# A weight split issued behind a later copy, DMA weight sums moved five products up, and branch A's block sums moved into the convolution stage

## The chip, the cores and the metric

The kernel runs on one core of one Trainium2 chip. The metric is device microseconds of one execution. The profile is of one execution, taken by the hardware profiler; its engines are PE (matmul), PEld (weight load), DVE, ACT, POOL and SP. SP and POOL only issue DMAs here, apart from two multiplies at the end on POOL.

## The reference, cut to what matters

One layer of a bidirectional encoder over 1024 tokens of width 1024, in float32:

```python
x = x + 0.5 * swiglu(rmsnorm(x, ffn1_norm), ffn1_w_in, ffn1_w_out)      # width 2816
h = rmsnorm(x, mix_norm)
z = h @ w_in                               # columns u, v | gate_b, gate_c, xb | g_a, g_b
u, v = gelu(u), gelu(v)
y_a = (u * (W_s rmsnorm(v) + b)) @ w_proj_a          # branch A
y_b = (gate_b * conv3(gate_c * xb)) @ w_proj_b       # branch B
x = x + (sigmoid(g_a) * y_a + sigmoid(g_b) * y_b) @ w_out
x = x + 0.5 * swiglu(rmsnorm(x, ffn2_norm), ffn2_w_in, ffn2_w_out)
return rmsnorm(x, final_norm)
```

## The kernel before, in words

Every large product is computed on feature-major activations (128 features x 512 tokens a tile, two token halves). A float32 factor is cut into a rounded part and a remainder (`parts`, line 85: an ACT copy makes `hi`, a DVE subtraction makes `lo`), and three matmuls of 128 x 512 replace one: hi*hi, hi*lo, lo*hi.

Products of a 2 x 2 block of weights with a 2 x 2 block of activations are taken by a Strassen-like scheme with seven products instead of eight. A **group** (`group`, line 352) is one such block: it runs its products in the order 1, 7, 6, 2, 5, 3, 4 (`ORDER`; `SHORT`, line 32, puts 4 ahead of 3 for blocks of fewer than four tiles), each of n*3 matmuls, n being 4, 3 or 2. Product 2 is cut in two halves around product 5 where n is 4. Three PSUM banks serve a group: `ba` takes product 1, then 6, 5 and 3 are added onto it one after the other, and after each an ACT copy takes the running sum out: `t1` after product 1, `u2` after product 6, `u5` after product 5. PE cannot add product 6 onto `ba` until the `t1` copy has read it, nor product 5 until the `u2` copy has, nor product 3 until the `u5` copy has.

**Weights.** `plan` lists all weight blocks ("S" entries; "F" entries are computed without the scheme, "R" are the last ones). An S entry loads raw tiles of 128 x 2 x 512 through SP (`fetch_until`): `x_`, `y_` and, unless its flag `dve` is set, `z_`. Five such buffers exist (tag "wr"). The seven weight factors are sums of blocks. For entries without the flag three accumulating DMAs on POOL's queue make them (`add_to`, line 94: y0 += x0, z0 += y0, z1 += y1); for entries with it (the second matrix of each feed-forward part, and the three projections) DVE makes two of the three. A fourth sum, x1 += z0, is always an accumulating DMA, issued once `pair(x_, 1, 2)` has read x_. Then `parts` splits each pair into `wh`/`wl` buffers (three of each), and the fourth sum alone into `wh4`/`wl4` (one of each), for product 3.

`make_ready` walks over all products of all entries (`units`) in the order in which they are used, `AHEAD` = 5 products ahead of the one that is taken, so the fourth sum's split, which belongs to product 3, stands in program order where product 1 of the same group is taken (in `ORDER`), and the three DMA sums of the next entry where product 6 of this group is taken. Program order is not queue order: a planner lays all instructions out by priority (program position, moved up by `high_priority`) over a simulated run, and an instruction that is ready there can come to stand in its engine's queue ahead of earlier ones that are not. Each engine's queue then runs in order.

**Stages.** In order: feed-forward 1 in (`gu`), out (`o`), then the mixer: `v`, `u`, eight `cx` and four `gb` groups (the convolution, lines 994 to 1040: `cx`, `cx`, `gb` for each d), eight `gg` groups (sigmoid gates, from line 1043), `ya`, `yb`, `o`, then feed-forward 2. Activations that a later stage needs in scheme form are put into DRAM tiles (`Shelf`). Branch A's shelf `ad` gets only its blocks when the gated heads are made (`gate_heads`, line 964); its sums are made later by `Shelf.sums` (line 684), a generator that loads four tiles, makes four differences on DVE and stores them, in five steps for each of four tiles k. Before the change its steps run in the first four `gg` groups, one after each product (lines 1050 and 1054). `Shelved` (line 703) loads the finished sums for the `ya` stage during `gg`. `unhurried` (line 312) issues gain and square work behind the `t1` copy.

Of the kernel before, what the change touches and what calls it, by code (L numbers as in the profile page):

```python
# [14 lines left out]
P = 128  # L15
# [20 lines left out]
def kernel(ctx, tc, x, ffn1_norm, ffn1_w_in, ffn1_w_out, mix_norm, w_in,  # L36
# [128 lines left out]
    AHEAD_OF = 300  # L165
    AHEAD = 5
    at = [0, 0, 0]
    raws, ready = {}, {}
    kept, closing = [], []

    def raw_tile():
# [2 lines left out]
    def fetch_until(e):  # L174
        while at[2] < min(e, len(plan)):
# [17 lines left out]
                nc.sync.dma_start(raw.rearrange("p h c -> p (h c)"), s[1][s[2] * P:(s[2] + 1) * P, :])  # L193
            at[2] += 1

    def make_ready(n):
        while at[1] < min(n, len(units)):
            e, i = units[at[1]]
            if i == 0 and not closing:
                return  # L200
            fetch_until(e + 1)
            s, q = plan[e], raws[e]
            if i == 0:
                f = s[2] - LAST
                if f % 2 == 0:
                    kept.append((big("wah", F32R), big("wal", F32R)))
                hi, lo = (t[:, (f % 2) * 2:(f % 2) * 2 + 2, :] for t in kept[-1])
                parts(hi, lo, q)
                ready[at[1]] = hi, lo
            elif s[0] == "F":  # L210
                c = i == "Y"
                if e == 1:
                    hi, lo = (t[:, 2 * c:2 * c + 2, :] for t in places(6))
                else:
                    hi = wp.tile([P, 2, HT], F32R, tag="wh", name=nm("wh"))
                    lo = wp.tile([P, 2, HT], F32R, tag="wl", name=nm("wl"))
                parts(hi, lo, q[c])
                ready[at[1]] = hi, lo
            else:
                if i == 1 and s[7]:  # L220
                    q.append(raw_tile())
                x_, y_, z_ = q
                sz = s[4] * P

                def pair(src, first, second):
                    hi = wp.tile([P, 2, HT], F32R, tag="wh", name=nm("wh"))
                    lo = wp.tile([P, 2, HT], F32R, tag="wl", name=nm("wl"))
                    with tc.high_priority(offset=AHEAD_OF // 2):
                        parts(hi[:, :, :sz], lo[:, :, :sz], src[:, :, :sz])
                    for h, name in enumerate((first, second)):  # L230
                        ready[e, name] = hi[:, h, :], lo[:, h, :]

                if i == 1:
                    if s[7]:
                        nc.vector.tensor_tensor(z_[:, 1, :sz], y_[:, 0, :sz], y_[:, 1, :sz], ALU.add)
                        nc.vector.tensor_tensor(z_[:, 0, :sz], z_[:, 1, :sz], x_[:, 0, :sz], ALU.add)
                        add_to(y_[:, 0, :sz], x_[:, 0, :sz])
                    else:
                        add_to(y_[:, 0, :sz], x_[:, 0, :sz])
                        add_to(z_[:, 0, :sz], y_[:, 0, :sz])  # L240
                        add_to(z_[:, 1, :sz], y_[:, 1, :sz])
                    pair(x_, 1, 2)
                    add_to(x_[:, 1, :sz], z_[:, 0, :sz])
                elif i == 6:
                    pair(z_, 6, 5)
                elif i == 7:
                    pair(y_, 7, 4)
                elif i == 3:
                    hi = wp.tile([P, HT], F32R, tag="wh4", name=nm("wh4"), bufs=1)
                    lo = wp.tile([P, HT], F32R, tag="wl4", name=nm("wl4"), bufs=1)  # L250
                    parts(hi[:, :sz], lo[:, :sz], x_[:, 1, :sz])
                    ready[e, 3] = hi, lo
                ready[at[1]] = ready.pop((e, i))
            if i in (0, 1, "X"):
                fetch_until(e + 2 + (i == 0))
            at[1] += 1

    def take(n, ahead=AHEAD):

# [92 lines left out]
    def group(name, blk, use, after=None):  # L352

        n = blk.n
        e, i = units[at[0]]
        assert i == 1 and plan[e][4] == n
        if after is None:
            after = lambda i: None
        asked = use

        def use(*args):
            with tc.high_priority(offset=AHEAD_OF):
                asked(*args)

        def tt(*args):
            with tc.high_priority(offset=AHEAD_OF):
                nc.vector.tensor_tensor(*args)

        def copy(*args):
            with tc.high_priority(offset=2 * AHEAD_OF):  # L370
                return nc.scalar.copy(*args)  # L371

        t1, u2, u5 = act("t1"), act("u2"), act("u5")

        def product(i, ps, first=True):
            w, = take(1)
            term(ps, w, blk, i, range(n), first)

        split = n // 2 if n == KH else n
        ba, bb_, bc = bank(name), bank(name), bank(name)  # L380
        product(1, ba)
        unhurried(copy(t1, ba))
        after(1)
        product(7, bb_)
        after(7)
        product(6, ba, False)
        copy(u2, ba)
        after(6)
        w2, = take(1)
        term(bc, w2, blk, 2, range(split))  # L390
        if split == n:
            u3 = act("u3")
            tt(u3, bb_, u2, ALU.add)
            use(0, 0, bc, t1)
            after(2)
        product(5, ba, False)
        copy(u5, ba)
        use(1, 1, bb_, u5)
        after(5)
        if split < n:  # L400
            term(bc, w2, blk, 2, range(split, n))
            use(0, 0, bc, t1)
            after(2)
        else:
            bd = bank(name)
            product(4, bd)
            use(1, 0, bd, u3)
            after(4)
        product(3, ba, False)
        use(0, 1, ba, None)  # L410
        after(3)
        if split < n:
            product(4, bb_, False)
            use(1, 0, bb_, u2)
            after(4)
# [578 lines left out]
    def conv_tile(d, cv):  # L994

        cx = big("cx")
        seen = set()

        def use(i, b, ps, add):
            s = cx[:, 2 * i + b, :]  # L1000
            if i == 0:
                scaled(s, i, ps, add, rb2[b])
            else:
                total(s, i, ps, add)
            seen.add((i, b))
            if (1 - i, b) in seen:
                nc.vector.tensor_tensor(cx[:, b, :], cx[:, b, :], cx[:, 2 + b, :], ALU.mult)

        group("cx", blk, use, after=lambda i: gate_heads() if i == 6 else None)
        ts = [cx[:, b, :] for b in range(NB)]  # L1010
        for b in range(NB):
            y = cv[:, 2 * (d // KH) + b, :]
            nc.vector.tensor_scalar(y, ts[b], gain(5, d), None, ALU.mult)
            for g, o, i in ((4, 1, 0), (6, 0, 1)):
                nc.vector.scalar_tensor_tensor(y[:, o:o + HT - 1], ts[b][:, i:i + HT - 1], gain(g, d),
                                               y[:, o:o + HT - 1], ALU.mult, ALU.add)
            if b > 0:
                nc.vector.scalar_tensor_tensor(y[:, 0:1], ts[b - 1][:, HT - 1:HT], gain(4, d), y[:, 0:1],
                                               ALU.mult, ALU.add)
            if b < NB - 1:  # L1020
                nc.vector.scalar_tensor_tensor(y[:, HT - 1:HT], ts[b + 1][:, 0:1], gain(6, d), y[:, HT - 1:HT],
                                               ALU.mult, ALU.add)
            nc.vector.tensor_tensor(y, y, rb[b], ALU.mult)

    for d in range(KH):
        cv = big("cv")
        conv_tile(d, cv)
        conv_tile(d + KH, cv)

        def use(i, b, ps, add):  # L1030
            y = cv[:, 2 * i + b, :]
            if add is None:
                nc.vector.tensor_tensor(y, ps, y, ALU.mult)
            else:
                s = act("gb")
                total(s, i, ps, add)
                nc.vector.tensor_tensor(y, s, y, ALU.mult)
            bd.put(i, b, d, y)

        group("gb", blk, use)  # L1040


    for d in range(ND):
        def use(i, b, ps, add):
            s = act("sig")
            scaled(s, i, ps, add, rb[b])
            nc.scalar.activation(s, s, AF.Sigmoid)
            nc.sync.dma_start((sad, sbd)[i][d][b], s)

        steps = ad.sums(d) if d < KH else iter(())  # L1050
        if d == ND - 3:
            nxt = Shelved(ad, "a")
        if d < ND - 1:
            group("gg", blk, use, after=lambda i: next(steps, None))
        else:
            last_group("gg", blk, use, nxt)
    blk = nxt
# [198 lines left out]
```

## Time and profile before

| | us |
|---|---|
| three runs | 2195.01, 2195.36, 2199.61 (median 2195.36) |
| the profiled execution | 2196.39 |
| its span, first to last instruction | 2194.6 |
| PE busy in it | 2121.6 (97%) |
| DVE, ACT busy | 1368.7 (62%), 921.1 (42%) |
| TensorE's mean granted clock | 0.987 |

PE is the engine that bounds the kernel; the others matter where PE waits for them. "DMA" in a windows table is the mean busy share of the 16 DMA engines; it can come out a little above 1. The name of a group of instructions is output<-inputs: `wh<-wr` is the cast of a raw weight tile, with 128x1024 for a pair and 128x512, 128x384 or 128x256 for the fourth sum of a block of four, three or two tiles; `wr<-wr` on POOL is a DMA weight sum; `L371 COPY t` is the `t1` copy, `L371 COPY u` that of `u2` or `u5`.

### The profile page before, as it was taken

What the parts mean: (1) busy time and instruction counts of PE and PEld (TensorE: products, weight loads), DVE (VectorE), ACT (ScalarE), POOL (GpSimd) and SP (SyncE); (2) the same over time, 40 slices, a digit from 0 to 9 for tenths busy, and PEclk for the clock granted to TensorE, in tenths of its full rate; (3) what the DMA queues carried; (4) which work ended last, traced back from release to release, by engine and by line L of the source; (5) the groups of instructions that cost most, each with busy time, mean ns of one, the idle gap of its engine ahead of it and who ended that gap; (6) DMA issues with size and microseconds to landing.
All of it is one profiled execution on the core that took longest, in us unless ns stands there. A gap on an engine that the chain in (4) does not pass through costs nothing. (4 is left out here: it accounts for less than half of the span.)

```text
span 2194.6 us, 27089 instructions
## 1 busy us (share of the span) xinstructions
PE 2121.6 (97%) x9374; PEld 1741.7 (79%) x9374; DVE 1368.7 (62%) x1930; ACT 921.1 (42%) x1350; POOL 418.0 (19%) x486
## 2 busy tenths in 40 slices
PE   7999999999999989999998999999999999999987
PEld 6788888878877878888886878877788888888876
DVE  5855656576476455766663568586765555576566
ACT  5533333355356553222233445355433333354444
POOL 2111111112222111111111101212111111112313
PEclk9999999999999999999999999999999999999999
DMA  9577777989898556677799799868577677997962
GB/s 273 125 202 182 184 187 179 257 257 246 180 234 202 126 120 169 149 167 164 172 339 240 200 292 297 204 182 201 128 197 197 172 199 175 261 238 176 205 188 77
DMA packets 451247, 435.98 MB, mean 199 GB/s; under 512 B 26860, under 2 KB 313636, under 8 KB 451108
## 3 DMA queue, kind: packets, MB, share of 16 engines
q1 hardware_dynamic: 385604, 315.20, 44.8%
q0 software_dynamic: 65504, 119.04, 32.2%
q8 instruction: 73, 1.20, 0.2%
q14 instruction: 66, 0.54, 0.1%
HBM read 235.43 MB, written 100.66 MB: 153 GB/s over the span
## 5 line engine op out<-in xcount | busy, mean ns | idle before, releaser
L87 DVE TENSOR_TENSOR wl<-wr,wh 128x1024 fp32r<-128x1024 f32 (+3 forms) x420 | 441.8, 1055 | 616.8 <-ACT wh L87 601.6
L87 ACT CAST wh<-wr 128x1024 fp32r<-128x1024 f32 (+3 forms) x420 | 383.4, 919 | 599.8 <-DMA wr<-wr 318.1
L95 POOL DMA_DIRECT2D wr<-wr x342 | 296.2, 906 | 1519.3 <-DVE wl L87 557.0
L371 ACT COPY u<-gu 128x512 f32<-128x512 f32 x82 | 47.8, 583 | 188.5 <-PE gu L83 188.5
L580 DVE TENSOR_TENSOR gu<-gu,rb 128x512 f32<-128x512 f32 x120 | 78.9, 685 | 0.0
L95 POOL DMA_DIRECT2D xd<-o x64 | 56.6, 954 | 103.7 <-DVE o L99 33.6
L99 DVE SCALAR_TENSOR_TENSOR gu<-gu,u 128x512 f32<-128x512 f32 x82 | 56.3, 687 | 12.7 <-PE gu L83 7.9
L371 ACT COPY u<-o 128x512 f32<-128x512 f32 x54 | 31.4, 582 | 74.2 <-PE o L83 70.8
L83 PE MATMUL gu<-t1h,wh 128*128 128x512 f32 x180 | 50.5, 393 | 8.8 <-ACT t1h L87 8.8
L739 ACT ACTIVATE gu<-gu 128x512 f32<-128x512 f32 x88 | 54.6, 627 | 7.3 <-DVE gu L580 7.3
L83 PE MATMUL gu<-t2h,wh 128*128 128x512 f32 x180 | 57.5, 394 | 0.0
L83 PE MATMUL gu<-t2l,wh 128*128 128x512 f32 x180 | 56.9, 390 | 0.5 <-DVE t2l L87 0.5
L742 DVE SCALAR_TENSOR_TENSOR gu<-gu,gu 128x512 f32<-128x512 f32 x88 | 57.3, 685 | 0.0
L83 PE MATMUL gu<-t2h,wl 128*128 128x512 f32 x180 | 56.7, 389 | 0.0
L83 PE MATMUL gu<-t3h,wh 128*128 128x512 f32 x180 | 50.3, 391 | 0.7 <-ACT u L371 0.6
L83 PE MATMUL gu<-t5h,wh 128*128 128x512 f32 x180 | 50.4, 391 | 0.0
L83 PE MATMUL gu<-t1l,wh 128*128 128x512 f32 x180 | 50.1, 390 | 0.0
L83 PE MATMUL gu<-t5l,wh 128*128 128x512 f32 x180 | 50.1, 389 | 0.0
L83 PE MATMUL gu<-t3l,wh 128*128 128x512 f32 x180 | 50.1, 389 | 0.0
L83 PE MATMUL gu<-t5h,wl 128*128 128x512 f32 x180 | 50.1, 389 | 0.0
L83 PE MATMUL gu<-t1h,wl 128*128 128x512 f32 x180 | 50.1, 389 | 0.0
L83 PE MATMUL gu<-t3h,wl 128*128 128x512 f32 x180 | 50.1, 389 | 0.0
(630 smaller groups left out, 5108.7 us busy)
## 6 DMA issues: line engine op xcount, KB each, us to landing
wr<-wr POOLq DMA_DIRECT2D x318, 256.0 KB, 4.7
wr<-in_ffn_w_in_dram SPq DMA_DIRECT2D x258, 256.0 KB, 4.3
wr<-in_w_in_dram SPq DMA_DIRECT2D x166, 256.0 KB, 4.3
gr<-g SPq DMA_DIRECT2D x140, 256.0 KB, 5.3
g<-ts SPq DMA_DIRECT2D x80, 256.0 KB, 4.6
xd<-o POOLq DMA_DIRECT2D x64, 256.0 KB, 6.0
g<-gu SPq DMA_DIRECT2D x60, 256.0 KB, 5.3
wr<-in_ffn_w_out_dram SPq DMA_DIRECT2D x48, 256.0 KB, 4.6
```

The costliest lines, as they stand in the source:

```text
L83: return nc.tensor.matmul(ps, l, r, start=start, stop=stop, skip_group_check=more)
L87: return nc.scalar.copy(hi, src), nc.vector.tensor_tensor(lo, src, hi.bitcast(F32), ALU.subtract)
L95: nc.gpsimd.dma_start(dst, src, accum_op=ALU.add)
L99: nc.vector.scalar_tensor_tensor(dst, a, -1.0, b, ALU.mult, ALU.subtract)
L371: return nc.scalar.copy(*args)
L580: nc.vector.tensor_tensor(dst, dst, rb, ALU.mult)
L739: nc.scalar.activation(s, s, AF.Silu)
L742: nc.vector.scalar_tensor_tensor(s, s, 0.5, u, ALU.mult, ALU.mult)
```

## The change

Three edits. The fourth sum's split is no longer issued by `make_ready`; it is kept in `late` and issued by `group` behind the copy of `u2`, with an edge of order on ACT (`tc.issue_after`). The three DMA sums of an entry go into `dma_sums`, which `make_ready` calls for the next entry where it splits `z_` (i == 6) of this one: five products earlier in program order; entries that follow another kind call it at i == 1 as before. Branch A's steps no longer run in the `gg` groups but in the `cx` and `gb` groups, after products 1, 5 and 3 of each group once `gate_heads` has run.

```diff
+    summed = set()
+
+    def dma_sums(e):
+
+        if e in summed:
+            return
+        summed.add(e)
+        x_, y_, z_ = raws[e]
+        sz = plan[e][4] * P
+        add_to(y_[:, 0, :sz], x_[:, 0, :sz])
+        add_to(z_[:, 0, :sz], y_[:, 0, :sz])
+        add_to(z_[:, 1, :sz], y_[:, 1, :sz])
...
+                if i == 1 and not s[7]:
+                    dma_sums(e)
...
                 elif i == 6:
                     pair(z_, 6, 5)
+                    if e + 1 < at[2] and plan[e + 1][0] == "S" and not plan[e + 1][7]:
+                        dma_sums(e + 1)
...
                 elif i == 3:
-                    hi = wp.tile([P, HT], F32R, tag="wh4", name=nm("wh4"), bufs=1)
-                    lo = wp.tile([P, HT], F32R, tag="wl4", name=nm("wl4"), bufs=1)
-                    parts(hi[:, :sz], lo[:, :sz], x_[:, 1, :sz])
-                    ready[e, 3] = hi, lo
-                ready[at[1]] = ready.pop((e, i))
+                    late[at[1]] = x_[:, 1, :sz]
+                if i != 3:
+                    ready[at[1]] = ready.pop((e, i))
...
+    def fourth_sum(ins):
+
+        (n, src), = late.items()
+        late.clear()
+        hi = wp.tile([P, HT], F32R, tag="wh4", name=nm("wh4"), bufs=1)
+        lo = wp.tile([P, HT], F32R, tag="wl4", name=nm("wl4"), bufs=1)
+        ready[n] = hi, lo
+        with tc.issue_after(ins.ins):
+            parts(hi[:, :src.shape[-1]], lo[:, :src.shape[-1]], src)
...
         product(6, ba, False)
-        copy(u2, ba)
+        fourth_sum(copy(u2, ba))
...
-        group("cx", blk, use, after=lambda i: gate_heads() if i == 6 else None)
+        group("cx", blk, use, after=mind_branch_a)
...
+    steps = (None for k in range(KH) for _ in ad.sums(k))
+
+    def mind_branch_a(i):
+        if todo and i == 6:
+            gate_heads()
+        elif not todo and i in (1, 5, 3):
+            next(steps, None)
+
...
-        group("gb", blk, use)
+        group("gb", blk, use, after=mind_branch_a)
...
-        steps = ad.sums(d) if d < KH else iter(())
...
-            group("gg", blk, use, after=lambda i: next(steps, None))
+            group("gg", blk, use)
```

## Rows read from the trace of the kernel before

**Rows 1.** The page, part 1: busy time, share of span, instructions.
```profile
PE 2121.6 (97%) x9374; PEld 1741.7 (79%) x9374; DVE 1368.7 (62%) x1930; ACT 921.1 (42%) x1350; POOL 418.0 (19%) x486
```

**Rows 2.** Waits of PE: us in total, times, longest.
```profile
PE o L83 <- ACT t L371: 11.2, 6, 3.6
...
PE gg L83 <- ACT t L371: 5.9, 2, 3.4
PE gg L83 <- ACT wh L87: 4.3, 1, 4.3
PE gu L83 <- ACT wh L87: 3.3, 1, 3.3
```

**Rows 3.** Windows: PE, PEld, DVE, ACT, POOL busy (instructions), granted clock, DMA, GB/s.
```profile
350.00:400.00 50.00, 50.00 (x222) 41.43 (x221) 29.86 (x41) 17.75 (x25) 7.76 (x9) 1.00 0.81 220
...
650.00:700.00 50.00, 46.37 (x197) 37.53 (x196) 29.83 (x36) 29.55 (x45) 16.14 (x19) 0.97 1.04 249
...
900.00:950.00 50.00, 50.00 (x222) 41.43 (x221) 30.99 (x46) 15.67 (x20) 8.91 (x11) 1.00 0.69 164
...
1100.00:1150.00 50.00, 49.79 (x220) 40.92 (x219) 31.79 (x45) 18.54 (x26) 6.87 (x8) 1.00 1.08 348
1150.00:1200.00 50.00, 39.79 (x157) 31.57 (x156) 17.93 (x23) 15.18 (x22) 8.71 (x11) 0.90 1.02 274
...
1500.00:1550.00 50.00, 46.42 (x193) 37.86 (x192) 40.44 (x51) 27.52 (x33) 12.14 (x14) 0.90 0.71 152
...
2050.00:2100.00 50.00, 46.50 (x198) 37.74 (x197) 31.89 (x48) 22.10 (x34) 15.39 (x18) 0.97 0.90 195
2100.00:2150.00 50.00, 46.22 (x226) 37.99 (x225) 29.78 (x40) 24.10 (x38) 5.54 (x5) 0.97 0.50 151
```

**Rows 4.** Timeline, feed-forward 1 out: start, us, engine, [idle before <-releaser].
```profile
658.37 1.13 POOL L95 DMA_DIRECT2D wr<-wr  x1
...
665.35 0.51 ACT L87 CAST wh<-wr 128x384 fp32r<-128x384 f32 x1 [8.50 <-DMA wr<-wr]
665.77 0.58 ACT L371 COPY t<-o 128x512 f32<-128x512 f32 x1
```

**Rows 5.** Timeline, where feed-forward 2 begins.
```profile
1526.56 0.62 ACT L87 CAST wh<-wr 128x512 fp32r<-128x512 f32 x1 [8.93 <-DMA wr<-wr]
...
1535.82 1.90 ACT L87 CAST t5h<-hr 128x2048 fp32r<-128x2048 f32 x1 [5.01 <-DVE hr L99]
...
1538.71 1.65 PE L83 MATMUL gu<-t7h,wh 128*128 128x512 f32 x3 [3.31 <-ACT wh L87]
```

**Rows 6.** Timeline of ACT, feed-forward 2 out.
```profile
2119.89 0.40 ACT L87 CAST wh<-wr 128x256 fp32r<-128x256 f32 x1 [5.35 <-DMA wr<-wr]
```

**Rows 7.** Timeline of the gg stage: SP's queue, POOL, ACT.
```profile
1150.43 3.38 SPq L719 DMA_DIRECT2D ar<-ad  x5
...
1162.51 1.73 POOL L95 DMA_DIRECT2D wr<-wr  x2 [12.44 <-DMA wr<-in_w_in_dram]
...
1171.33 1.04 ACT L87 CAST wh<-wr 128x1024 fp32r<-128x1024 f32 x1 [7.17 <-DMA wr<-wr]
```

**Rows 8.** The gg tile, one product: ns min/median/max, first and last start.
```profile
L83 PE MATMUL gg<-t1h,wh x32: 389/389/390, 1101.0 to 1250.6; 128*128 128x512 f32 x32
```

**Rows 9.** Timeline of an undisturbed gu cycle, feed-forward 2.
```profile
1672.97 0.85 POOL L95 DMA_DIRECT2D wr<-wr  x1 [4.70 <-DVE wl L87]
1674.93 6.27 SPq L183 DMA_DIRECT2D wr<-in_ffn_w_in_dram  x6
1676.40 0.62 ACT L87 CAST wh<-wr 128x512 fp32r<-128x512 f32 x1 [3.28 <-DMA wr<-wr]
...
1684.92 0.88 POOL L95 DMA_DIRECT2D wr<-wr  x1 [4.52 <-DMA wr<-in_ffn_w_in_dram]
1686.12 0.59 ACT L371 COPY u<-gu 128x512 f32<-128x512 f32 x1 [4.85 <-PE gu L83]
...
1691.11 1.06 ACT L87 CAST wh<-wr 128x1024 fp32r<-128x1024 f32 x1 [0.28 <-PE gu L83]
```

More of the change, by code (lines that the diff above doesn't have):

```diff
@@ L167 @@
     at = [0, 0, 0]
-    raws, ready = {}, {}
+    raws, ready, late = {}, {}, {}
     kept, closing = [], []
@@ L237, in make_ready @@
                         add_to(y_[:, 0, :sz], x_[:, 0, :sz])
[L238 to L241, printed above, removed]
                     pair(x_, 1, 2)
@@ L1038, in use @@
             bd.put(i, b, d, y)
-        group("gb", blk, use)
+        group("gb", blk, use, after=mind_branch_a)
+    assert next(steps, "end") == "end"
     for d in range(ND):
```

## The prediction, made before the change was run

> **What bounds the kernel now.** I read the page first: PE is busy 97% of the span [rows 1], so a gain has to come out of PE's idle time and out of stretches where its matmuls run slowly. The waits of PE come second. Those this change can touch are four: 11.2 us in six waits of the `o` products on the `t1` copy, 5.9 and 4.3 us in `gg` on the `t1` copy and on a weight split, and 3.3 us in `gu` on a weight split [rows 2]. In all of them the one waited for is ACT, an engine that is busy 42% [rows 1]: it is late because it stands in order behind something, not because it is full. The third view, the windows of 50 us, prices the waits fully. An undisturbed window holds 222 matmuls, 0.225 us each, at granted clock 1.00 [rows 3]; the window 1150 to 1200 holds 157 at 0.90, so 65 are lost, 14.6 us, where the waits in it are 10.2 us. The rest is the clock: a window at 0.90 ran 5.0 us short of full-speed time, one at 0.97 1.5 us [rows 3]. So the longer of these waits also cost a stretch at the lower level (1.2 GHz) behind them, and that cost goes with the wait.
>
> The fourth view, the timeline of ACT, names what it stands behind. In `o`, ACT sat 8.50 us before the split of a fourth sum (128x384) until an accumulating DMA landed, and the `t1` copy, which needed nothing of it, came right behind at 665.77 [rows 4]. The DMA was issued at 658.37, so issue to landing was some 7 us. The split at 2119.89 had waited 5.35 us in the same way [rows 6]. Where feed-forward 2 begins, the split at 1526.56 waited 8.93 us with block casts queued behind; the last of their chain, t5h, came at 1535.82, and PE waited 3.3 us for the weight cast behind it [rows 5]. In `gg` the sums themselves are late: POOL waited 12.44 us for a weight load while SP was issuing shelf loads, and a pair's split waited 7.17 us [rows 7].
>
> **Edit 1, the fourth split behind the u2 copy.** It adds no instruction; it moves one ACT cast and one DVE subtraction in each of some 100 groups. ACT's queue then has `t1` and `u2` ahead of the DMA's landing.
> - `o` stages: the 11.2 us of waits on the `t1` copy are of this kind [rows 2], and the three windows at 0.97 with such waits give 3 x 1.5 = 4.5 us of clock [rows 3]: 15.7. What is late next is `u2`: in feed-forward 1 some eight gain and square activations stand between the two copies, so I take 0.8 back: -14.9. Bounds: nothing (the wait turns up at `u5` or product 3) and -15.7.
> - Start of feed-forward 2: the 3.3 us wait and 5.0 us of clock in its window [rows 2, 3]: -8.3, if the block casts run in the 8.93 us that ACT sat idle [rows 5]. What could be late next is the weight pair behind them, whose buffers come free only with the whole group's end. Bounds 0 and -8.3; I take the whole, as the 8.93 us are more than twice the 3.3.
> - The new wait: product 3 waits for the split; `u5`, the next entry's pair casts and the stage's activations are queued behind it on ACT, the remainder's subtraction and what follows it on DVE. From the `u2` copy to product 3 lie product 5 and half of product 2, 18 matmuls, 4.1 us, where the split takes 0.62 [rows 9] and a like subtraction. Landing 7 us after issue [rows 4] falls ahead of or near the `u2` copy. Bounds 0 and +1.3 us (cast and subtraction uncovered) in a late group; I take 4 such groups: +5.
> - The buffer: `x_` is held until the split. In an undisturbed cycle the split is at 1676.40 and the `u2` copy of the same group ends at 1686.71 [rows 9], so one of five raw buffers comes free 10.3 us later, and one load of the six issued from 1674.93 on moves there. Its cover: the last of these loads is issued by 1681.20 and releases POOL at 1684.92, 3.7 us; an add from issue at 1672.97 to the cast that it releases takes 3.4 us [rows 9]. Issued at 1687.5, behind the remainder, the load is landed at 1691 and summed by 1696. Its pair is cast one cycle (84 matmuls, 18.9 us) after 1691.11 [rows 9], at 1710: 14 us are left. I take 0; without cover see the third rival.
>
> **Edit 2, DMA sums five products sooner.** Nothing is added: three adds on POOL's queue get an earlier place in about 65 groups. In the undisturbed cycle they already start when their load lands (POOL at 1684.92 is released by a load [rows 9]), so there it is worth 0. They may come to stand ahead of the fourth add in POOL's in-order queue and hold it until a load lands; the longest kind of wait for a load seen in `gg`, 12.44 us [rows 7], is about what edit 1 has given the fourth split. Bounds -3 (the short waits in `gg`) and +3; I take 0, and count its help in `gg` with edit 3.
>
> **Edit 3, branch A's sums during the convolution.** Moved: 4 x 4 loads and 4 x 4 stores of 256 KB, 8.4 MB, all on SP's queue, and 16 DVE operations. They leave the first four `gg` groups, from 1101.0 on [rows 8], and go into about seven of the twelve `cx`/`gb` groups ahead of it (20 steps, three a group): seven groups of 18.9 us, 132 us. `gg` from 1100 to 1200 ran at DMA share 1.08 and 1.02, the convolution at 0.69 [rows 3]. Without them SP has only gates, weights and branch A's shelf loads in `gg`, and the 14.6 us of its worst window go: -14.6. Bounds 0 and -15.2 (waits 10.2 plus clock 5.0).
> What it costs there: 8.4 MB over 132 us is 64 GB/s. Between the windows at 164 GB/s, share 0.69, and at 348 GB/s, share 1.08 [rows 3], a GB/s costs 0.0021 of share: the convolution rises to 0.83. A window at 0.81 and 220 GB/s ran with PE at 50.00 of 50 [rows 3], so I take 0. Bounds 0 and +14.6 (all that `gg` lost is lost there). DVE's 16 operations of 128x512 lie beside its 31 of 50 [rows 3]. The sums' tile takes one of 18 big buffers, 14 of which hold block parts; `cv` and at most two `cx` leave it one, and I take 0 for that too.
> A rule speaks against this edit. The Trainium skill (DMA: Bandwidth & Descriptors, section Issuing engines are not separate DMA queues) says that transfers run on the same 16 engines and interleave, whichever engine began them. By it the moved blocks slow the convolution's weight loads and POOL's sums too, and a move only changes the place of the loss; the sum would then lack the 14.6. The trace of `gg` agrees that the sharing hurts at 1.08, and the full window at 0.81 that it need not below; I go by the windows.
>
> **The sum.** -14.9 - 8.3 - 14.6 = -37.8; new waits +5, and +1 left of the `gg` stalls: -31.8. The profiled execution took 2196.39 us (span 2194.6 and 1.8 around it), 1.0 above the median of 2195.36. 2196.4 - 31.8 = 2164.6, as a median about **2164 us**, 1.4% less.
>
> **Rivals.**
> 1. The convolution takes over what `gg` lost. For: SP's queue is in order, and a store that waits for its DVE difference holds weight loads behind it, as in `gg`. Against: 0.81 ran clean [rows 3]. 2164 + 14.6: 2179.
> 2. The split is moved but its DMA is later still, so `u5` and product 3 wait and half of the `o` and feed-forward 2 terms stay. For: 5 to 9 us idle ahead of these splits [rows 4 to 6]. Against: 4.1 us more room plus the time of two products. 2164 + 11.6: 2176.
> 3. Slower: the raw ring starves. `x_` held 10.3 us longer delays a load in each group without DVE sums; it is covered by 14 us, so it decides from the point where a load and its add come 14 us later than in the undisturbed cycle. POOL's 12.44 us wait for a load shows that it can get close [rows 7], and the convolution now has the added traffic. Price: three late `gg` groups cost 14.6, 4.9 each; if ten of the twenty convolution and gate groups fall late, +49 in place of `gg`'s present loss: 2196.4 - 37.8 + 49 - 1 = 2207. Against: the undisturbed stages keep 14 us.
> 4. It does not do what it says: the planner has its own order, the splits stand so late in it already in most groups (and DMA sums at their loads [rows 9]) that only places are exchanged, and other splits (a pair's, as in [rows 7]) now stand ahead of the `t1` copy: 2196.
>
> **Chances.** Forecast 0.56 (own range 2152 to 2175), rival 1 0.14, rival 2 0.10, rival 3 0.11, rival 4 0.09. The range 2149 to 2195 takes in the forecast and rivals 1 and 2 with the bounds of the terms, and about half of rival 4; what is left out is rival 3, half of 4 and a few hundredths below. A measurement of this kernel can tell 0.2%, 4.4 us, from no change: faster than 2191.0 takes in the forecast and rivals 1 and 2, 0.79 with their tails taken off; within it rival 4, 0.10; slower 0.11.
>
> **What would show it.** Right: in the timeline of ACT the `t1` copies follow product 1 by about the 0.2 us of a free engine, and each 128x512 (or x384, x256) cast stands behind a `COPY u`; the row "PE o <- ACT t" falls from 11.2 to under 2; the window of the end of `gg` holds about 220 matmuls at clock 1.00 with DMA share under 0.9; the convolution's windows keep 222 with a share near 0.83; t5h at the start of feed-forward 2 comes some 7 us sooner relative to its group. Wrong: waits of PE on `wh` or `wl` with product 3, a `cx` or `gb` row among the waits of PE, POOL waiting longer for loads in total, or ACT's copies still behind a pair's split.

## The result, and the profile after

The changed kernel took 2173.76 us (median of 4 runs, 2168.75 to 2175.68) beside 2196.44 us of the kernel before: medians 22.7 us apart, 1.0%. The ratio on record is 0.9878 [0.9859, 0.9898], which is 26.8 us (22.4 to 31.0), 1.2%; it is not the quotient of the two medians, and the tables below go by such ratios. The time lies within the range, 9.8 us above the predicted 2164, at the upper end of the forecast's own range (2152 to 2175). The profiled execution took 2174.83 us, with a span of 2173.0. In the changed kernel the copies `t` and `u` are line 392 (371 before), the VectorE sums of the weights lines 250 and 251 (235 and 236 before).

First the page's busy times, which answer to [rows 1]: PE lost 10 us of busy time with the same 9374 matmuls, because fewer of them ran at the lower clock: 70 matmuls started some 0.2 us later behind the one ahead than at full speed in the kernel before, 37 in the changed one.

```profile
PE 2111.4 (97%) x9374; PEld 1737.5 (80%) x9374; DVE 1367.6 (63%) x1930; ACT 925.3 (43%) x1350; POOL 420.5 (19%) x486
```

The waits of PE of the changed kernel (us in total, times, longest) answer to [rows 2]:

```profile
PE o L83 <- ACT wah L87: 5.2, 1, 5.2
PE o L83 <- ACT wh L87: 4.5, 1, 4.5
...
PE o L83 <- ACT u L392: 4.4, 9, 1.1
PE o L83 <- DVE wl L87: 4.3, 4, 2.8
PE yb L83 <- ACT t L392: 2.3, 1, 2.3
...
PE gg L83 <- ACT u L392: 0.3, 1, 0.3
```

All four rows that the prediction went after are gone: there is no row "o <- ACT t" (11.2 us before), none of `gu` on a weight split (3.3), and neither of the two of `gg` (10.2); the 0.3 us of `gg` on `u` was 0.6 before. But three rows of `o` that were 0.7 us (`wah`), absent (`wh`) and 2.9 us (`wl`) stand at 5.2, 4.5 and 4.3, and one of `yb` went from 0.3 to 2.3. The windows of 50 us of the changed kernel (busy and instructions of PE, PEld, DVE, ACT, POOL; granted clock; DMA share; GB/s) answer to [rows 3]:

```profile
650.00:700.00 50.00, 47.46 (x209) 38.64 (x208) 33.41 (x42) 33.42 (x51) 15.65 (x19) 1.00 1.04 250
900.00:950.00 50.00, 50.00 (x223) 41.38 (x222) 37.94 (x59) 14.61 (x19) 8.67 (x10) 1.00 0.96 253
950.00:1000.00 50.00, 50.00 (x222) 41.42 (x221) 36.31 (x57) 14.54 (x20) 8.93 (x10) 1.00 0.90 242
...
1100.00:1150.00 50.00, 50.00 (x222) 41.39 (x221) 21.94 (x29) 18.92 (x28) 8.64 (x10) 1.00 1.05 301
1150.00:1200.00 50.00, 50.00 (x223) 41.39 (x222) 24.75 (x32) 21.69 (x31) 10.44 (x12) 1.00 0.81 197
...
1500.00:1550.00 50.00, 50.00 (x226) 40.97 (x225) 37.01 (x60) 23.37 (x29) 10.48 (x12) 1.00 0.64 137
2050.00:2100.00 50.00, 45.54 (x191) 37.15 (x190) 35.63 (x59) 20.70 (x36) 9.46 (x11) 0.93 0.84 226
2100.00:2150.00 50.00, 44.34 (x221) 37.24 (x221) 31.96 (x76) 27.70 (x51) 17.21 (x12) 0.97 0.23 85
```

Read them against [rows 3]: the end of `gg` (1150 to 1200) went from 157 matmuls at clock 0.90 to 223 at 1.00, the start of feed-forward 2 (1500 to 1550) from 193 at 0.90 to 226 at 1.00, and 650 to 700 from 197 to 209. The convolution (900 to 1000) still holds 222 and 223 with the added transfers. The windows from 2050 on hold other work than before, since the changed kernel is over 20 us ahead there, and cannot be held against [rows 3]. Matmul by matmul, from 2046 us of the changed kernel to its end, it gained 9.9 us and lost 12.5.

### The profile page after: what moved, and what is told of

It is laid out like the page before. It is cut to its first block, busy times and chain, and to the rows that moved or that the text cites. A ratio compares the mean times of both kernels' runs of the same rounds, so it can differ in the third digit from the quotient of the medians.

```text
span 2173.0 us, 27092 instructions
## 1 busy us (share of the span) xinstructions
PE 2111.4 (97%) x9374; PEld 1737.5 (80%) x9374; DVE 1367.6 (63%) x1930; ACT 925.3 (43%) x1350; POOL 420.5 (19%) x486
## 4 chain that ended last, share of the span: by engine, by line
PE 76%; DVE 7%; DMA 7%; issue 5%; ACT 4%; SPq 1%; POOL 1%; DVEq 0%; POOLq 0%; ACTq 0%
PE gu L83 36%; PE o L83 14%; PE cx L83 7%; PE gg L83 7%; PE gb L83 4%; PE u L83 3%; PE v L83 2%; PE ya L83 2%; DMA gr<-g 1%; DMA wr<-in_ffn_w_out_dram 1%; DVE wl L87 1%; PE sgu L83 1%; PE yb L83 1%; DMA gr<-gd 1%; DMA wr<-wr 1%
## 5 line engine op out<-in xcount | busy, mean ns | idle before, releaser
L392 ACT COPY u<-o 128x512 f32<-128x512 f32 x54 | 31.4, 582 | 84.2 <-PE o L83 81.7
L392 ACT COPY t<-gu 128x512 f32<-128x512 f32 x41 | 24.1, 588 | 70.8 <-PE gu L83 70.8
```

## The experiments

In all twelve experiments the time is compared with the kernel before on the same chip; us are (1 - ratio) times its median (2198.34, 2198.72 and 2197.55 us in the three sets of four).

| kernel | median us | ratio to before | us |
|---|---|---|---|
| all three edits (the change) | 2173.76 | 0.9878 [0.9859, 0.9898] | -26.8 |
| e1_split | 2191.36 | 0.9967 [0.9954, 0.9981] | -7.3 |
| e2_sums | 2197.11 | 0.9992 [0.9981, 1.0002] | -1.8 |
| e3_branch | 2182.69 | 0.9937 [0.9920, 0.9955] | -13.8 |
| e13 | 2177.61 | 0.9906 [0.9891, 0.9921] | -20.7 |
| split_t1 | 2163.42 | 0.9839 [0.9826, 0.9851] | -35.4 |
| hold | 2193.97 | 0.9981 [0.9969, 0.9992] | -4.2 |
| end | 2173.15 | 0.9878 [0.9865, 0.9890] | -26.8 |
| dbl_a | 2176.54 | 0.9894 [0.9880, 0.9908] | -23.3 |
| t1_yb | 2164.06 | 0.9838 [0.9816, 0.9861] | -35.6 |
| t1_yb_end | 2160.13 | 0.9819 [0.9795, 0.9842] | -39.8 |
| e1_t1 | 2179.89 | 0.9911 [0.9893, 0.9930] | -19.6 |
| e13_t1 | 2167.97 | 0.9857 [0.9836, 0.9879] | -31.4 |

**Which edit gives what.** Four kernels take the change apart.

e1_split, the first edit alone (the fourth sum is left to `fourth_sum`, called behind the copy `u2`):

```
...
                 elif i == 3:
...
-                    parts(hi[:, :sz], lo[:, :sz], x_[:, 1, :sz])
...
+                    late[at[1]] = x_[:, 1, :sz]
...
-        copy(u2, ba)
+        fourth_sum(copy(u2, ba))
```

> Edit 1 alone: the fourth sum's split behind the u2 copy, everything else as before. My theory: the waits of PE on the t1 copy in the o stages (11.2 us) and the 3.3 us at the start of feed-forward 2 go with their clock loss, some -20 to -25; about 10 us come back as weights that are late in the o stages, because a raw buffer is held some 10 us longer; the gg stage keeps its losses (PE waits there stay above 6 us). So 2181 to 2188 against 2196.4, ratio 0.993 to 0.996. Rival A (the gg gain of the whole change is edit 1's, since one of the gg waits was also on a t1 copy behind a split): gg waits of PE fall under 3 us and the time is 2172 to 2178. Rival B (any edit reshuffles the planner's order and the parts do not add up): no forecast of place; stalls appear where neither kernel had any.

e2_sums, the second edit alone:

```
...
-                        add_to(y_[:, 0, :sz], x_[:, 0, :sz])
-                        add_to(z_[:, 0, :sz], y_[:, 0, :sz])
-                        add_to(z_[:, 1, :sz], y_[:, 1, :sz])
...
                     pair(z_, 6, 5)
+                    if e + 1 < at[2] and plan[e + 1][0] == "S" and not plan[e + 1][7]:
+                        dma_sums(e + 1)
```

> Edit 2 alone: the three DMA sums of the next entry five products sooner in program order. My theory: the sums are started by the landing of their loads, not by program order, so nothing: 2194 to 2198, ratio 0.999 to 1.001, POOL's adds in the undisturbed gu cycle at the same places. Rival: they were late by order, above all in gg: gg waits of PE fall by a third or more, 2188 to 2192. Rival B (reshuffle): a change of more than 4 us either way with stalls at new places.

e3_branch, the third edit alone:

```
...
-        group("gb", blk, use)
+        group("gb", blk, use, after=mind_branch_a)
...
-            group("gg", blk, use, after=lambda i: next(steps, None))
+            group("gg", blk, use)
```

> Edit 3 alone: branch A's block sums in the convolution groups. My theory: the gg stage loses its waits (10.2 us) and their clock, -13 to -15, the convolution stays at 222 matmuls a window with DMA share 0.85 to 0.97: 2181 to 2184, ratio 0.993 to 0.994. Rival A (the gg gain needs edit 1): less than -7, 2190 or more, with a wait on a t1 copy left in gg. Rival C (the convolution takes the loss over): a cx or gb row among the waits of PE, 2190 to 2197.

e13, the first and the third together, without the second:

> Edits 1 and 3 without edit 2. My theory: the time of the whole change, 2170 to 2176, within 3 us of it. If edit 2 is needed for what the others give (sums that come late once the raw buffers are held longer): 2178 or more, with new waits on weight splits in gu, cx or gg.

Measured: -7.3, -1.8 (not told from nothing), -13.8 and -20.7 us; the first and the third add up (21.1). e1_split's 0.9967 is a little short of the 0.993 to 0.996 expected, and e13 stands 6 us from the change where 3 were expected. The second edit alone is not told from nothing; with the others the ratios with and without it are 0.9878 and 0.9906, intervals that overlap. The waits of PE of e3_branch and then of e1_split show which loss belongs to which edit:

```profile
PE o L83 <- ACT t L371: 13.1, 6, 4.7
...
PE gg L83 <- ACT t L371: 1.1, 1, 1.1
```

```profile
PE gg L83 <- ACT wh L87: 7.8, 1, 7.8
PE o L83 <- ACT wah L87: 5.4, 1, 5.4
PE o L83 <- DVE wl L87: 4.8, 5, 2.4
...
PE gg L83 <- ACT t L379: 3.6, 1, 3.6
PE yb L83 <- ACT t L379: 3.3, 1, 3.3
```

The loss in `gg` goes with the third edit and with nothing else: e1_split has 7.8 and 3.6 us there, and its window 1150 to 1200 holds 156 matmuls. The late `t` copies of `o` go with the first edit and stay without it. And the rows that grew in the changed kernel (`wah`, `wl`, `yb`) stand already in e1_split: the first edit makes them. The fourth, `o <- ACT wh`, is 1.2 us there and 4.5 in the change.

**Is it the raw buffer?** The first edit lets the fourth sum's raw buffer go only after the copy `u2`. Two kernels change the time of holding. hold leaves ScalarE's order as it is; split_t1 also moves the split ahead of `u2` on ScalarE, and its remainder on VectorE with it.

split_t1, the fourth sum split behind the copy `t`, two products sooner:

```
-        unhurried(copy(t1, ba))
+        first = copy(t1, ba)
+        unhurried(first)
...
         product(7, bb_)
+        fourth_sum(first)
...
-        fourth_sum(copy(u2, ba))
+        copy(u2, ba)
```

> The changed kernel with one difference: the fourth weight sum is split behind the copy of the first sum of products (t) and no longer behind the copy of the third (u), one or two products (1.4 to 5.4 us) sooner. Theory of the buffer: the late split holds its raw buffer longer, the loads of the next weights start later, and that is what the stalls of about 2.5 us at 505 us and 4.6 us at 2067 us of the changed kernel are; with the split sooner they shrink to under 1 us each, no wait of the stages "o" for ACT t returns (the split is still behind that copy), and the time is 4 to 9 us below that of the changed kernel, a ratio to the kernel before of 0.984 to 0.986. Rival, the place on ScalarE: the stalls have nothing to do with the buffer, the split in front of the copy u waits for its running sum as it did in front of t in the kernel before, waits for ACT u of 4 to 10 us in all appear, and the ratio is 0.989 to 0.993.

hold, the changed kernel with a reader of the raw half (which `fourth_sum` returns) one and a half products later:

```
...
+        return src
...
-        fourth_sum(copy(u2, ba))
+        held = fourth_sum(copy(u2, ba))
...
         use(1, 1, bb_, u5)
+        tt(small("held", 1), held[:, :1], u5[:, :1], ALU.add)
```

> The changed kernel with one addition: a VectorE addition of one column, behind the copy u5 of each group, that reads the raw half of the fourth sum and so holds the buffer about 5 us longer (two products), while ScalarE's order stays as it is. Theory of the buffer: raw buffers are the scarce thing in the stages that make their sums on VectorE ("o", "ya", "yb"), so the stalls at 505 and 2067 us grow by 2 to 5 us each and new ones of the same kind (VectorE or ScalarE waiting for a weight load, TensorE for wl or wh) appear in several groups: 10 to 30 us in all, a ratio of 0.992 to 1.001. Rival: there is cover enough, the buffer was not the cause, and the ratio stays at 0.987 to 0.990.

Measured: split_t1 is 8.6 us faster than the change, hold 22.6 us slower. The waits of VectorE for weight loads in feed-forward's second halves (us in total, times, longest), from the kernel before, split_t1, the change and hold, rise in the order of the holding time:

```profile
DVE wr L235 <- DMA wr<-in_ffn_w_out_dram: 4.0, 2, 3.7
```

```profile
DVE wr L250 <- DMA wr<-in_ffn_w_out_dram: 11.9, 3, 9.5
```

```profile
DVE wr L250 <- DMA wr<-in_ffn_w_out_dram: 20.8, 6, 9.9
```

```profile
DVE wr L250 <- DMA wr<-in_ffn_w_out_dram: 67.5, 20, 8.0
```

In hold, SP's weight loads waited 84 times for the reader that was added (in the change they wait for the remainders `wl`, 204 times):

```profile
SPq L183 <- DVE held L389: 601.5, 84, 19.2
```

So a buffer that is held longer starts its loads later, and the stages that sum on VectorE pay for it. VectorE works in order, so a sum that waits for its load (line 250) keeps the `wl` of the product at hand behind it; PE's row "o <- DVE wl" is 10.2 us in hold and 4.3 in the change.

At the two places that split_t1's expectation names, however, something else ended the wait last. The first, from the timeline of the changed kernel (start, us, engine, [idle before <-releaser]):

```profile
481.40 8.28 SPq L740 DMA_DIRECT2D gr<-g  x9
481.85 0.59 ACT L392 COPY t<-o 128x512 f32<-128x512 f32 x1 [1.67 <-PE o L83]
487.29 0.59 ACT L392 COPY u<-o 128x512 f32<-128x512 f32 x1 [4.85 <-PE o L83]
487.78 0.62 ACT L87 CAST wh<-wr 128x512 fp32r<-128x512 f32 x1
488.43 0.69 DVE L87 TENSOR_TENSOR wl<-wr,wh 128x512 fp32r<-128x512 f32 x1 [5.42 <-ACT wh L87]
491.11 3.85 SPq L183 DMA_DIRECT2D wr<-in_ffn_w_out_dram  x4
504.97 0.69 DVE L250 TENSOR_TENSOR wr<-wr 128x512 f32<-128x512 f32 x1 [9.85 <-DMA wr<-in_ffn_w_out_dram]
```

and the same place in the kernel before:

```profile
482.28 0.62 ACT L87 CAST wh<-wr 128x512 fp32r<-128x512 f32 x1 [2.57 <-DMA wr<-wr]
484.03 17.12 SPq L183 DMA_DIRECT2D wr<-in_ffn_w_out_dram  x8
496.08 0.69 DVE L235 TENSOR_TENSOR wr<-wr 128x512 f32<-128x512 f32 x1 [3.70 <-DMA wr<-in_ffn_w_out_dram]
```

Before, the split came when its sum landed (482.28), the first load was issued at 484.03, and the sum on VectorE ran at 496.08. Now the split waits for `u` (487.78), the first load is at 491.11, the sum on VectorE at 504.97, and PE waits 2.8 us for the `wl` behind it. (The cast behind `COPY u`, and the `t` copy at 481.85 with nothing ahead of it, are what the prediction asked the timeline to show.) But the buffer was free at 489.12, when the remainder was made. SP issued gate loads (`gr<-g`) until 489.68, and what its load at 491.11 waited for last was the landing of one of these:

```profile
SPq L183 <- DMA gr<-g: 1.4, 1, 1.4
```

In the five kernels with the split behind `t` this split starts at 482.6 to 484.1, about as in the kernel before, yet the first load came at 485.5 to 490.8, and PE still waited 2.3 to 4.8 us. So this part of the expectation failed: a shorter hold does not mend this place. The gate loads took 8.0 us from issue to landing between 480 and 505 in the change and 10.1 before, where PE didn't wait, so their slowness alone is not the cause either; it stays open.

The other place, 2067 us, did go: the row "o <- ACT wh", 4.5 us, is absent in split_t1. Its rows in the changed kernel, and then in split_t1:

```profile
2060.49 0.42 DVE L251 TENSOR_TENSOR wr<-wr,wr 128x256 f32<-128x256 f32 x1
2064.46 0.86 POOL L95 DMA_DIRECT2D wr<-wr  x1 [0.45 <-DVE xs L840]
2071.73 1.14 ACT L87 CAST wh<-wr 128x512 fp32r<-128x512 f32 x2 [7.24 <-DMA wr<-wr]
```

```profile
2056.39 0.42 DVE L251 TENSOR_TENSOR wr<-wr,wr 128x256 f32<-128x256 f32 x1
2058.02 0.85 POOL L95 DMA_DIRECT2D wr<-wr  x1 [2.96 <-DVE t3l L87]
```

VectorE's sums waited for no load here in either kernel. The split, that of a pair here, waited for an accumulating DMA, which POOL issued 1.6 us after the start of VectorE's sum in split_t1 and 4.0 us after it in the change, behind two other accumulating DMAs of its queue (`xd<-o`, the outputs). That is order in queues, and no late load. e1_split, with its split in the same place, lost only 1.7 us here. So hold shows that the time of holding has a price; how much of the gain of split_t1 is the buffer, and how much the order behind the split, stays open. The rival had a part: the waits for the copy `u` in `o` rose from 4.4 to 8.0 us (6.6 before), since the split now stands ahead of it; the gain is net of that.

e1_t1 makes the same move with the first edit alone, e13_t1 takes the second edit out of split_t1.

> The kernel before with the first edit alone, but with the fourth sum split behind the copy t and not behind u. Theory of the buffer: the hold of the raw buffer, one to two products longer than need be, cost the first edit 8 to 10 us of what it had taken away; so this is 15 to 18 us below the kernel before, a ratio of 0.992 to 0.9935, against 0.9967 for the first edit as it was made (e1_split). Rival: split_t1's gain comes from how the sooner split stands to the earlier DMA sums (second edit) or to branch A (third); then this comes out as e1_split did, 0.995 to 0.998.

> split_t1 without the second edit (the DMA sums begun five products sooner). If the second edit does nothing, as alone (0.9992), this is split_t1 again, a ratio of 0.983 to 0.985. If it is needed once the first edit holds buffers longer (the first and third edits without it gave 0.9906, all three 0.9878), the ratio is 0.986 to 0.988, with waits of the stages gu, v or gg for weights that are late.

Measured: e1_t1 -19.6 us where e1_split gave -7.3. So two products of delay cost the first edit 12 us, without any help of the other edits; it did a little better than the 15 to 18 expected. e13_t1 has 0.9857 beside split_t1's 0.9839, intervals that overlap and come from two chips: for the second edit nothing is shown, though both comparisons lean to a gain, of 4 and 6 us.

**Has the convolution room?** dbl_a issues each of the moved loads twice:

```
             for o, i in ((0, 12), (2, 3)):
                 nc.sync.dma_start(t[:, o, :], self.td[i][k])
+                nc.sync.dma_start(t[:, o, :], self.td[i][k])
             yield
             for o, i in ((1, 1), (3, 2)):
+                nc.sync.dma_start(t[:, o, :], self.td[i][k])
                 nc.sync.dma_start(t[:, o, :], self.td[i][k])
```

> The changed kernel with one addition: each load of branch A's block sums during the convolution is issued twice into the same place, 16 more loads of 256 KB (4.2 MB) between about 890 and 1080 us. Theory that the transfers of the convolution have room: at a mean DMA share of 0.96 TensorE still ran full there (222 to 223 matmuls in 50 us), so the addition costs 0 to 2 us, a ratio of 0.987 to 0.989. Rival, the convolution is at its limit: 4.2 MB at the 250 GB/s that these windows move are 17 us of transfer, part of which TensorE waits for: 5 to 15 us, a ratio of 0.990 to 0.995, with new waits of the stages cx and gb.

Measured: 0.9894, between the figures of theory and rival. The change's interval holds it, so by the time a cost of some 3 us can't be excluded; but the windows of the convolution in dbl_a stay full with more moved in them:

```profile
900.00:950.00 50.00, 50.00 (x222) 41.45 (x221) 37.45 (x57) 15.43 (x20) 8.70 (x10) 1.00 1.01 276
950.00:1000.00 50.00, 50.00 (x223) 41.41 (x222) 36.45 (x56) 13.15 (x18) 8.70 (x10) 1.00 0.99 275
```

No row of `cx` or `gb` stands among PE's waits. What hides the transfers is slack, not speed: PE runs full although the loads land later. Weight loads in 890 to 1080 us took 3.5 us from issue to landing before, 4.5 after and 4.8 in dbl_a. The rows are those of the kernel before, then of the change (issues, KB each, median us to landing):

```profile
wr<-in_w_in_dram SPq DMA_DIRECT2D x60, 256.0 KB, 3.5
wr<-wr POOLq DMA_DIRECT2D x40, 256.0 KB, 3.9
```

```profile
wr<-in_w_in_dram SPq DMA_DIRECT2D x61, 256.0 KB, 4.5
wr<-wr POOLq DMA_DIRECT2D x40, 256.0 KB, 5.3
```

**Why the last groups gave nothing.** The loss at a place is summed here over the distances between neighbouring matmuls' starts, each less 226 ns. In the kernel before, PE lost 2.6 us at 2118 us to the `t` copy of [rows 6], and 1.7 more at the lower clock behind it. That is gone, and at the transposes that follow the loss rose by 6.1 us (to the 10.9 that the expectation below names): from the first of them to the first product with `wah` it took 9.3 us before and 14.4 after, and more matmuls ran at the lower clock behind it. ACT's timeline there, before and after:

```profile
2123.86 1.91 ACT L87 CAST gh<-gr 128x2048 fp32r<-128x2048 f32 x1
...
2133.24 3.06 ACT L1173 COPY xs<-xT 128x512 f32<-128x512 f32 x6
2136.09 1.14 ACT L87 CAST wah<-wr 128x1024 fp32r<-128x1024 f32 x1
```

```profile
2102.30 1.91 ACT L87 CAST gh<-gr 128x2048 fp32r<-128x2048 f32 x1 [2.13 <-DMA gr<-gd]
2104.11 3.99 ACT L1203 COPY xs<-xT 128x512 f32<-128x512 f32 x8
...
2114.00 3.95 ACT L87 CAST wah<-wr 128x1024 fp32r<-128x1024 f32 x4
```

The gates' first load `gr` was issued at 2116.63 before and at 2093.68 after; the first product with `wah` started at 2137.28 and 2115.17: 20.7 and 21.5 us. This is a chain of its own (load, split, copies behind the transposes, split of `wah`) that starts when PE has read a block for the last time. The old wait of PE at 2118 lay beside that chain, not on it, so its end brought nothing. The kernel end puts the splits of `wah` ahead:

```
...
         closing.append(True)
+        last_ws.extend(take(NF - LAST))
         for b in range(NB):
...
-    ws = take(NF - LAST)
+    ws = last_ws
```

> The changed kernel with one difference at its end: the four splits of the last output weights (wah, 128x1024) stand on ScalarE ahead of the splits of the gates (gh) and the copies behind the transposes. Theory of the chain at the end: from the release of the gates' buffer to the first product with wah ScalarE is a chain of 21 us in the kernel before and in the changed one alike, and so the removal of the late copies t in the last groups of "o" (4.8 and 4.3 us) came back as 9.2 us at the transposes; with 3.8 us of splits out of that chain the loss there falls from 10.9 to 6 to 9 us and the time by 2 to 4 us, a ratio of 0.986 to 0.987. Rival: the gates' loads land too late, whatever stands in front of them; the loss stays at 10 to 11 us and the ratio at 0.988.

Measured: no gain, 0.9878. The stretch from the first transpose to the first product with `wah` fell to 10.7 us, but `gr`, which now takes a later buffer, is issued at 2102.17, and the copies of the last groups stand behind the `wah` splits (1.0 and 1.7 us lost). The rival was wrong about the loss, which fell, and right about the time.

**The boundary of `yb`, and the best version.** In split_t1 the copy `t` of the last `yb` group stands behind a split that waits for the running sum:

```profile
1392.34 1.47 ACT L87 CAST t1h<-mr 128x1536 fp32r<-128x1536 f32 x1 [7.16 <-DMA mr<-sl]
1393.72 0.58 ACT L392 COPY t<-yb 128x512 f32<-128x512 f32 x1
```

That is the fault that the first edit mends, in another place. t1_yb is split_t1 with the two turned around (cut):

```
+            if name == "yb" and i == 1:
+                with tc.issue_after(at_t[0].ins):
+                    nxt.make(1, a, z)
```

> The kernel with the fourth sum split behind the copy t (split_t1), and one more difference: at the last group of "yb" the split of the next blocks (t1h, 128x1536, which waits for the running sum of the last products) stands on ScalarE behind the copy t and no longer in front of it. Theory: the 4.1 us (and 2.5 at a lower clock) that TensorE stood there at 1390 us in split_t1 are that order alone, t1h waiting 7.2 us for its data with the copy t behind it; they fall under 1 us, nothing else moves, and the time is 4 to 7 us below split_t1's, a ratio of 0.981 to 0.9825. Rival: the copy t was waiting for something else as well, or the split of t1h, now later, holds up the first group of the next stage by as much; the ratio stays at 0.983 to 0.985.

```profile
1390.93 0.59 ACT L392 COPY t<-yb 128x512 f32<-128x512 f32 x1 [2.57 <-PE yb L83]
1394.67 1.48 ACT L87 CAST t1h<-mr 128x1536 fp32r<-128x1536 f32 x1 [3.16 <-DMA mr<-sl]
```

The wait is gone (3.9 us in split_t1, no row of `yb` here), and the window 1350 to 1400 holds 222 matmuls in place of 193. The time doesn't show it: 0.9838 beside 0.9839, the rival's figure and not the 0.981 to 0.9825 expected. In the profiled execution 6.6 us went at `yb`, and 3.1 us more were lost near 501 us (a stall of 4.9 us, 2.6 in split_t1, with the clock behind it); the interval is 10 us wide. With end's edit added:

> The kernel t1_yb with the splits of the last output weights (wah) ahead of those of the gates, as in the kernel end. Theory: the end is a chain on ScalarE, of which 3.8 us go, while two copies of the last group of "o" wait behind the earlier splits: end showed a loss of 5.6 us in place of 10.9 at the transposes, but 1.0 and 1.7 us new in the group before and no time gained that could be measured. So 0 to 3 us below t1_yb, a ratio of 0.980 to 0.9825. Rival: the earlier splits cost as much as they give, and the ratio is that of t1_yb within 0.0005.

Measured: 0.9819 [0.9795, 0.9842], the fastest of all, 39.8 us below the kernel before. It beats the change beyond the intervals; that it beats split_t1 does not follow.

## Why the prediction was right, and where its sizes were off

- **The first edit's waits.** Forecast -14.9 in `o` and -8.3 at the start of feed-forward 2, together -23.2. Summed by place as above, in the profiled executions, e1_split lost 25 us less than the kernel before at these places: 6.9 at 630 to 672 us, 7.9 at the start of feed-forward 2, 3.1 and 4.3 in the last groups, 3.0 at 1451 to 1461. The mechanism was right; the clock's price came out with the waits. One reservation: e3_branch, without the first edit, waited only 1.4 us for `wh` at the start of feed-forward 2, and 220 matmuls stand in its window; so that part is not the edit's alone. The sign named for it, t5h some 7 us sooner relative to its group, did not come: t5h starts 7.4 us ahead of the group's `t` copy in both kernels.
- **The step that was mis-sized: the new waits, +5, with "The buffer: [...] I take 0".** e1_split gave back some 17 us: 6.6 at the end, 4.3 at 503 us, 2.9 at `yb`, the rest in pieces of about 1 us (3.0 us are lost at 701, but the kernel before lost 2.0 there too). The working named what is queued behind the split but priced only the wait of product 3. None of these places is a wait of product 3, and none is shown to be the buffer: the end is the chain described above, `yb` is a copy behind a block split, and the stall at 503 stays when the hold is shortened. What had no price is that other instructions on ScalarE, VectorE and POOL come to stand in another order when the split moves. That two products less of delay bring 8.6 and 12.3 us (split_t1, e1_t1) is shown, the share of the buffer in it is not.
- **The cover of the buffer.** The 14 us were read in one undisturbed `gu` cycle and carried to every stage. hold shows where that does not carry: VectorE's waits for loads of the second feed-forward matrices rise to 67.5 us and the time by 22.6 us, while PE has no row of `cx`, `gb` or a weight wait of `gg`.
- **The last groups.** [rows 6] were priced as if PE's wait there were on the path. About 4 us of the -14.9 could not be had, as the chain of 21 us at the end shows.
- **The second edit.** 0 forecast, -1.8 [-4.2, +0.4] alone.
- **The third edit.** -14.6 forecast, -13.8 [-17.6, -9.9] measured, and nothing paid in the convolution. By place `gg` gave 13.4 us in e3_branch; another 5.6 came at the start of feed-forward 2, and about as much was lost in small pieces elsewhere, so that the total fits so well is in part chance. The share rose to 0.96 and 0.90 in the convolution and not to 0.83: the steps ran from 885 to 969 us, 84 us and not 132 (the window 1000 to 1050 is back at 0.72 and 160 GB/s), so 164 GB/s became 253. The rule of the Trainium skill (DMA: Bandwidth & Descriptors, section Issuing engines are not separate DMA queues), that transfers interleave on the same 16 engines whichever engine began them, agrees with the landing times: with the moved transfers on SP's queue, weight loads begun by SP went from 3.5 to 4.5 us and POOL's sums from 3.9 to 5.3. What the prediction drew from it as a rival, that the loss would only change its place, did not come about.
- **The rivals.** The first (the convolution takes over the loss) and the fourth (nothing) did not come about. The third did not come about in the change; hold brings on something like it, in `o` and not in the convolution or `gg`; POOL's waits for weight loads, a sign of it, fell in total (`in_ffn_w_in` from 305.4 to 107.4 us, `in_w_in` from 179.9 to 128.1). The second's time, 2176, is nearer to the measured one than the forecast's 2164, so the time does not decide against it; the rows do: PE waits nowhere for the weights of product 3, and "o <- ACT u" fell from 6.6 to 4.4 us.

The sum from the measured parts: -7.3 - 1.8 - 13.8 = -22.9 beside -26.8 for the whole, within the intervals. By place, in the two profiled executions (21.6 us apart), the change gained some 20 us in `o` (14.9 forecast), 7.9 at the start of feed-forward 2 (8.3) and 14.8 in `gg` (14.6), and some 21 came back where 6 were forecast (6.4 at 2067 us, 6.1 at the end, 3.6 at `yb`, 3.1 near 501). So the forecast was low because of what came back, and no lower only because `o` gave more than its term; that offset is luck.

## What to carry to other kernels

When an instruction is moved later, price also what stands behind it on each queue and what it holds: the buffer that it frees starts a load (one and a half products more of holding cost 22.6 us in hold), and the cover for that load has to be read in the tightest stage that uses the ring, not in a quiet one. Put such an instruction behind the first thing that it used to delay and no further; here two products of extra delay gave back 12 of 20 us. And ask of each wait near a chain's end whether something longer runs beside it before its whole length is booked.

## What was not expected of the hardware

- A mean DMA share of 1.05 at 301 GB/s (1100 to 1150 us after), and 1.01 and 0.99 in dbl_a, with 222 or 223 matmuls at clock 1.00. In `gg` before, 1.08 and 1.02 went with the loss; the share alone did not tell a disturbed window from an undisturbed one. [rows 7] have SP issuing shelf loads while POOL waits 12.44 us for a weight load; that the order in SP's queue was the cause, and not the amount moved, no run here shows separately.
- In the changed kernel a wait of 4.6 us at 2067.6 us was followed by twelve matmuls that together took 2.5 us more than 226 ns each; its window (2050 to 2100) ran at a granted clock of 0.93 with 191 matmuls. With the wait gone in split_t1, the 50 us up to 2090, which end before the transposes, hold 215 at 1.00.
